# Two units of half products: the second unit's sums of weights made during the first, kept in DRAM, and its additions shared

## The chip, the cores and the metric

One core of one Trainium2 chip runs the whole layer as one program. The metric is the device time of one execution in microseconds (us). Engines are named as in the profile: PE is TensorE (PEld its weight loads), DVE is VectorE, ACT ScalarE, POOL GpSimd, SP SyncE, which here does nothing but issue DMAs ("SPq" is its queue).

## The reference

One layer of a hybrid encoder: D = 1024 channels, T = 1024 + 128 = 1152 tokens. Two branches, an SSD (Mamba-2) branch `y_m` of width 2048 and an attention branch `y_a` of width 1024, are projected to 1024 channels, gated, summed, projected again and normalised:

```python
u = gate_m * jnp.einsum('ble,ed->bld', y_m, w_br_m) + gate_a * jnp.einsum('ble,ed->bld', y_a, w_br_a)
out = jnp.einsum('bld,de->ble', u, w_out)
x_new = layer_norm(DN_ALPHA * x + out, ln_g, ln_b)
```

The change concerns these three lines only, the last 420 us of the kernel. What stands before them (input projection, convolution, scan, attention) is the same in both kernels.

## The kernel before

**Numbers in two halves.** All products are of 32-bit accuracy: each operand is split into a high part `h` (a cast on ACT) and a low part `l` (the difference, on DVE or POOL), and three matmuls (h·h, h·l, l·h) make one product. A matmul is 128 x 128 weights by 384 tokens; the tokens lie in three chunks c0, c1, c2 of 384.

**Order of the last part.** `quarter(A0)`: the first half of `y_a` times its weights. `unit(0)`: rows 4 to 11 of `y_m` (in tiles of 128 rows). `quarter(A1)`: the second half of `y_a`. `unit(1)`: rows 0 to 3 and 12 to 15 of `y_m`. Then the output projection with w_out, chunk by chunk (`out`), with the LayerNorm behind each block.

**A unit** is a product in Strassen's manner. Chunks c0 and c1 and the two halves of the unit's rows make the 2 x 2 blocks; seven products do the work of eight. The blocks of weights for output pair (j1, j2) = (2p, 2p + 1) are B11, B21, B12, B22 and the sums T1, T2, T4, T3; the right sides are A11, A12, A22 and the sums S1 to S4. Chunk c2 is done plainly (D1, D2) with the B pieces. For each p, of which a unit has four (0 to 3 in unit 0; 4 to 7 in unit 1, where the loop variable is again 0 to 3 and the diff says p), that is 11 products of 12 matmuls. So a unit has 528 matmuls. The order of the eight pieces is a table, `ORDERS`, chosen for each p by `PIECES`. The results are added into `acc`, up to four places for one product, on DVE (in unit 0 the first touch of a place is a copy on ACT).

**Weights.** `load_pair` loads the two tiles of 512 KB (B11 and B21; B12 and B22) on SP. `prepare` makes a piece `pc` (1024 wide, high and low half side by side) three pieces ahead of its use: for a T the sum, in place, on DVE (on POOL for the very first p), then the cast on ACT, then the low half on POOL. After T4 and T3 the loads of the next p are issued into the same two raw tiles, so they wait for the POOL subtraction that read them last. `pc` tiles live in the rotating slots `wh` and `wl`, the raw tile B11/B21 in the slot `wr`, which ordinary weights (`fetch`, `split`) use as well.

**What sets the order.** Each engine runs its instructions in the order in which the program lists them, and in the units that is the order of the code (`manual_schedule`). `flow` is a generator ticked every 6 matmuls; its `yield n` waits n ticks. In unit 0 it runs `rows_c01` (loads the second half of `y_a` and splits its chunks c0 and c1 into `ya1hi`, `ya1lo`; `rows_c2` does chunk c2), in quarter 1 `load_sums(1)` (loads unit 1's rows, scales them and makes the sums S), in unit 1 `seconds` (loads the attention product `pa`, its second half and its gate, adds and scales). `final` loads the SSD gate and `finish` multiplies and adds on DVE and POOL; `parts_of_u` splits the merged result into `uhi`, `ulo`; `load_late` and `late` do the same for chunk c2. `load_wo` and `split_wo` load and split the eight rows of w_out; the first two come through `fetch` and `split`. Products of quarter 1 go through a tile `pa` to DRAM (`evac_1`).

Of the kernel before, what the change touches and what calls it, by code (L numbers as in the profile page):

```python
# [19 lines left out]
P = 128  # L20
# [6 lines left out]
CW = 384  # L27
# [122 lines left out]
def trunk_step(ctx: ExitStack, tc: tile.TileContext, I, O):  # L150
# [1194 lines left out]

    def load_sums(v):

# [4 lines left out]
        rb = [None]  # L1352
        pair_ = [send(kts[0], rb, *(() if v else (lazy["f0"], "gs"))), send(kts[1], rb)]
        for i in range(4):
            y0, y1 = pair_
            scaled(kts[2 * i], y0, rb)
            scaled(kts[2 * i + 1], y1, rb)
            if i < 3:
# [24 lines left out]
            if i >= 2:  # L1383
# [4 lines left out]
              ("B11", "B21", "T1", "T2", "B12", "B22", "T4", "T3"))  # L1388
    PIECES = [ORDERS[i] for i in (0, 1, 1, 1, 0, 1, 1, 2)]
    raw = {}  # L1390

    def load_pair(p, which):

        if p % 4 or which >= 2:
            which %= 2
            pool, tag = ((wp, "wr"), (lazy["raw"], "raw"))[which]
            raw[p, which] = t = pool.tile([P, 1024], F32, tag=tag, name=f"wu{p}_{which}", bufs=1)
            sy.dma_start(t[:], I["wbr"][4 + 2 * p + which + 4 * (p // 4)])

    pieces = []  # L1400

    def prepare():

        n = len(pieces)
        if n >= lazy["limit"]:
            return
        p, name = n // 8, PIECES[n // 8][n % 8]
        j1, j2 = raw[p, 0], raw[p, 1]
        b11, b21, b12, b22 = j1[:, 0:512], j1[:, 512:1024], j2[:, 0:512], j2[:, 512:1024]
        out = {"B11": b11, "B21": b21, "B12": b12, "B22": b22, "T1": b11, "T2": b11, "T4": b21, "T3": b12}[name]  # L1410
        if name[0] == "T":
            x, y = {"T1": (b12, b11), "T2": (b22, b11), "T4": (b21, b11), "T3": (b22, b12)}[name]
            (ve if p else po).tensor_tensor(out, x, y, ALU.subtract)  # L1413
        t = wp.tile([P, 1024], F32R, tag=("wh", "wl")[n % 2], name=f"pc{n}")
        ac.copy(t[:, 0:512], out)  # L1415
        po.tensor_tensor(t[:, 512:1024], out, t[:, 0:512].bitcast(F32), ALU.subtract)  # L1416
# [17 lines left out]
    def unit(v, steps):  # L1434

        def to(j, c, d):
            a = acc[:, j, ch(c)]
            if v == 0 and (j, c) not in begun:
                begun.add((j, c))
                ac.copy(a, d)  # L1440
            else:
                ve.tensor_tensor(a, a, d, ALU.add)

        begun = set()
        for p in range(4):
# [11 lines left out]
            for at, piece in enumerate(order):  # L1457
# [51 lines left out]
    lazy["sub"] = po  # L1509
    A1 = [tuple(ap.tile([P, 4, CW], F32R, tag=f"a{x}{c}", name=f"ya1{x}{c}") for x in ("hi", "lo")) for c in range(2)]  # L1510
    ys = []

    def part(i, c):
        h, l = A1[c][0][:, i, :], A1[c][1][:, i, :]
        ac.copy(h, ys[i][:, ch(c)])
        ve.tensor_tensor(l, ys[i][:, ch(c)], h.bitcast(F32), ALU.subtract)

    def rows_c01():

        yield 20  # L1520
        for i in range(4):
            y = mp.tile([P, T], F32, tag="yr", name=f"yr1{i}", bufs=4)
            sy.dma_start(y[:], ya_d[4 + i])
            ys.append(y)
            yield 5
            part(i, 0)
            yield 3
            part(i, 1)
            yield 3

    def rows_c2():

        A1.append(tuple(ap.tile([P, 4, CW], F32R, tag=f"a{x}2", name=f"ya1{x}2") for x in ("hi", "lo")))
        for i in range(4):
            part(i, 2)

    def steps_0(p, piece):

        if p == 3 and piece == "B22":
            flow.after(1, rows_c2)  # L1540

# [77 lines left out]
    def load_wo(*ks):  # L1619

        for k in ks:
            pool, tag = {2: (ap, "ahi1"), 3: (ap, "alo1"), 4: (ap, "ahi0"), 5: (ap, "alo0")}.get(k, (mp, "yr"))
            wraw[k] = pool.tile([P, 1024], F32, tag=tag, name=f"wor{k}", bufs=1 if k < 6 else 4)
            sy.dma_start(wraw[k][:], I["w_out"][k])

    def split_wo(k):

        where = {5: "2", 6: "1", 7: "0"}.get(k)
# [4 lines left out]
        wo.append((hi, lo))  # L1633

    def steps_1(p, piece):

        a, b = 2 * p, 2 * p + 1
        at = PIECES[4 + p].index(piece)
        if p:
            if 1 <= at < 4:  # L1640
                finish(1)
            if at < 4:
                final(((a - 2, 0), (b - 2, 0), (a - 2, 1), (b - 2, 1))[at])
            if at == 4:
                finish(1)
            if at == 6:
                finish(len(pending))
            if at == 7 and p < 3:
                flow.start(seconds(p + 1))
        if p == 2 and at == 0:  # L1650
            load_wo(2, 3)
# [23 lines left out]
    op = ma_stack.enter_context(tc.tile_pool(name="op", bufs=1, reuse_waits="tile"))  # L1675
    last_w = ready.pop(0)
    split()
    wo += [last_w, ready.pop(0)]
    split_wo(2)
    final((6, 1), (7, 1))  # L1680
    gb = xp.tile([P, 2, D], F32, tag="xhi2", name="gb")
    sy.dma_start(gb[:, 0, :], I["ln_g"].to_broadcast([P, D]))
    sy.dma_start(gb[:, 1, :], I["ln_b"].to_broadcast([P, D]))
    for c in range(NCH):
        xr = xp.tile([P, 3, D], F32, tag="xlo2", name=f"xres{c}")
        sy.dma_start(xr[:], I["xt"][3 * c * P:(3 * c + 3) * P].rearrange("(j p) d -> p j d", p=P))
# [7 lines left out]
        def product(j, n, at):  # L1694
# [5 lines left out]
            d = ds[j, n]  # L1700
            (wh, wl), k = wo[at], at
            te.matmul(d[:, :w], uh[:, k, js], wh[:, ns], start=(at == 0), stop=False)
# [3 lines left out]
        if c == 0:  # L1706
            for k in range(8):
                for j, n in blocks:
                    product(j, n, k)
                if k < 5:  # L1710
                    split_wo(k + 3)
                if k == 0:
                    finish(2)
                    load_late(0)
                if k > 1:
                    late(k - 2)
# [116 lines left out]
```

## Time and profile before

| | us |
|---|---|
| median of 3 runs (lowest to highest) | 2038.79 (2038.76 to 2039.94) |
| the profiled execution | 2038.8 |
| its span | 2037.0 |
| quarter 0, 1616.95 to 1666.94 | 49.99 |
| unit 0, to 1758.77 | 91.83 |
| quarter 1, to 1813.80 | 55.03 |
| unit 1, to 1915.66 | 101.86 |
| output c0, c1, c2, to 2029.85 | 41.49, 32.66, 40.04 |
| tail | 7.15 |

The stages are cut where TensorE's matmuls pass from one line of the kernel to the next. In profile lines, `out<-in` are the program's names without their numbers, `x3` is a count, and `[1.18 <-ACT wh L225]` says that the engine had been idle for 1.18 us and what ended that. `L246` is a line of the kernel.

### The profile page before, as it was taken

The numbers are of one execution on the slowest core, as the hardware profiler recorded it, in microseconds if no ns is written. First come the engines' busy times: TensorE is split into PE (matmuls) and PEld (weight loads), VectorE is DVE, ScalarE is ACT, GpSimd is POOL, SyncE is SP. The second block draws the span as 40 slices with busy tenths as digits, with TensorE's granted clock in tenths as the row PEclk, the third lists the DMA queues.
The fourth block names the chain that finished last, engine by engine and source line by source line (L and its number), as shares of the span: only waits on it lengthen the run. The fifth ranks groups of instructions, "written<-read, shape, count | busy, mean of one in ns | idle before, by whom it ended". The sixth has DMA issues, their size and how long they took to land.

```text
span 2037.0 us, 36365 instructions
## 1 busy us (share of the span) xinstructions
PE 2007.6 (99%) x14199; PEld 1858.2 (91%) x14199; DVE 1351.3 (66%) x2233; ACT 949.2 (47%) x2055; POOL 557.8 (27%) x732
## 2 busy tenths in 40 slices
PE   9999999999999999999999999999999999999897
PEld 7899999999999999999888888888988999989786
DVE  4145666666767667643678778777787675577876
ACT  5125455465565555543545554544555453341310
POOL 0012535453545454432010010001001025325610
PEclk9999999999999999999999999999999999999998
DMA  6423242324233332434456665656667662455652
GB/s 221 165 66 97 65 136 79 131 79 128 91 125 91 118 116 82 142 105 164 160 182 214 202 192 192 196 213 198 187 216 207 215 224 100 156 183 196 217 171 93
DMA packets 131691, 311.39 MB, mean 153 GB/s; under 512 B 19528, under 2 KB 78912, under 8 KB 121280
## 3 DMA queue, kind: packets, MB, share of 16 engines
q1 hardware_dynamic: 113936, 217.78, 33.4%
q10 hardware_dynamic: 17584, 91.30, 13.0%
q8 instruction: 111, 1.82, 0.4%
q14 instruction: 60, 0.49, 0.1%
HBM read 243.07 MB, written 65.95 MB: 152 GB/s over the span
## 4 chain that ended last, share of the span: by engine, by line
PE 80%; DVE 9%; DMA 6%; ACT 2%; issue 1%; POOL 1%; SPq 0%; ACTq 0%; DVEq 0%; POOLq 0%
PE d L246 17%; PE d L248 16%; PE d L247 16%; PE s L952 3%; PE o L1027 2%; PE y L737 2%; PE v L336 2%; PE v L335 2%; PE v L334 2%; PE so L1102 1%; PE dS L678 1%; PE y L741 1%; PE ss L1080 1%; PE dq L247 1%; PE dq L246 1%
## 5 line engine op out<-in xcount | busy, mean ns | idle before, releaser
L246 PE MATMUL d<-xh,wh 128*128 128x384 f32 x2112 | 736.2, 349 | 0.0
L248 PE MATMUL d<-xh,wl 128*128 128x384 f32 x2112 | 708.3, 335 | 0.0
L247 PE MATMUL d<-xl,wh 128*128 128x384 f32 x2112 | 707.2, 335 | 0.0
L246 PEld LDWEIGHTS d<-xh,wh 128*128 128x128 f32 x2112 | 396.6, 188 | 19.0 <-issue 7.9
L247 PEld LDWEIGHTS d<-xl,wh 128*128 128x128 f32 x2112 | 397.2, 188 | 0.8
L248 PEld LDWEIGHTS d<-xh,wl 128*128 128x128 f32 x2112 | 396.4, 188 | 0.0
L226 POOL TENSOR_TENSOR wl<-wr,wh 128x1024 fp32r<-128x1024 f32 x37 | 89.0, 2404 | 189.1 <-ACT wh L225 189.1
L1416 POOL TENSOR_TENSOR pc<-wu,pc 128x512 fp32r<-128x512 f32 x64 | 87.9, 1381 | 172.8 <-ACT pc L1415 172.8
L957 ACT ACTIVATE st<-s,ckt 128x256 f32<-128x256 f32 (+1 forms) x320 | 115.1, 467 | 19.6 <-PE s L952 17.3
L1017 ACT ACTIVATE st<-st 128x1024 f32<-128x1024 f32 x80 | 83.1, 1062 | 41.6 <-DVE st L1012 38.4
L961 POOL TENSOR_TENSOR st<-st,mask_bf 128x256 f32<-128x256 f32 x64 | 48.8, 783 | 194.4 <-ACT st L957 194.3
L706 ACT ACTIVATE m<-ce,nacum 128x128 f32<-128x128 f32 x288 | 96.8, 391 | 5.7 <-PE y L737 5.7
L1415 ACT CAST pc<-wu 128x512 fp32r<-128x512 f32 x64 | 38.5, 622 | 116.8 <-DVE wu L1413 88.9
L229 DVE SCALAR_TENSOR_TENSOR wl<-wr,wh 128x1024 fp32r<-128x1024 f32 x50 | 62.1, 1242 | 32.5 <-ACT wh L228 32.4
L633 POOL TENSOR_TENSOR wx<-xdt,wdt 128x256 f32<-128x256 f32 x72 | 54.0, 751 | 84.9 <-DVE xdt L631 84.9
L225 ACT CAST wh<-wr 128x1024 fp32r<-128x1024 f32 x48 | 50.3, 1049 | 53.7 <-PE d L247 43.9
L1027 PE MATMUL o<-st,vt 128*64 128x256 f32 (+1 forms) x640 | 68.9, 362 | 0.9 <-ACT st L1017 0.4
L1027 PEld LDWEIGHTS o<-st,vt 128*64 128x64 f32 x640 | 43.4, 137 | 26.7 <-ACT st L1017 4.0
L852 ACT ACTIVATE gate<-d,bcol 128x384 f32<-128x384 f32 x48 | 27.7, 578 | 71.9 <-PE d L248 46.7
L686 POOL TENSOR_TENSOR S<-S,ea 128x256 f32<-128x256 f32 x56 | 37.8, 674 | 75.9 <-DVE S L687 64.6
L1038 DVE TENSOR_TENSOR st<-st 128x1024 f32<-128x1024 f32 (+1 forms) x40 | 57.4, 1436 | 0.8
L228 ACT ACTIVATE wh<-wr 128x1024 fp32r<-128x1024 f32 x50 | 52.7, 1054 | 10.7 <-PE d L247 10.7
(906 smaller groups left out, 4324.8 us busy)
## 6 DMA issues: line engine op xcount, KB each, us to landing
wr<-in_wt SPq DMA_DIRECT2D x88, 512.0 KB
kc<-in_cache_k ACTq DMA_DIRECT2D x32, 1024.0 KB
vc<-in_cache_v ACTq DMA_DIRECT2D x32, 1024.0 KB
ce<-ac_d SPq DMA_DIRECT2D x96, 192.0 KB
sb<-cs_d ACTq DMA_DIRECT2D x16, 576.0 KB
yr<-ym_d SPq DMA_DIRECT2D x16, 576.0 KB
gate_d<-gate SPq DMA_DIRECT2D x45, 192.0 KB
s<-in_state_ssm SPq DMA_DIRECT2D x8, 1024.0 KB
```

Of the source, the lines that this page charges most:

```text
L226: lazy.get("sub", po).tensor_tensor(lo[:, :cols], raw[:, :cols], hi[:, :cols].bitcast(F32), ALU.subtract)
L229: ve.scalar_tensor_tensor(lo[:, :cols], raw[:, :cols], scale, hi[:, :cols].bitcast(F32), ALU.mult, ALU.subtract)
L246: te.matmul(out, wh, xh, start=(k == 0), stop=False)
L247: te.matmul(out, wh, xl, start=False, stop=False)
L248: te.matmul(out, wl, xh, start=False, stop=(k == n - 1))
L706: ac.activation(m[:, j, :], ce[:, j * P:(j + 1) * P], AF.Abs, bias=nacum[:, b, h:h + 1])
L952: te.matmul(ps2[:, e, 256 * x + q0:256 * x + 256], kk[hr, ks], qq[hr, qs], start=(at == 0), stop=(at == 2))
L957: ac.activation(S[j][:, e, kb, q0:], ps2[:, e, 256 * x + q0:256 * x + 256], AF.Identity, bias=ckt[:, kb, 2 * hp + e:2 * hp + e + 1])
L1017: ac.activation(w, w, AF.Exp, scale=-1.0)
L1027: te.matmul(o[64 * e:64 * e + 64, 256 * at + q0:256 * at + 256], vt[:, kb, 64 * e:64 * e + 64], S[j][:, e, kb, q0:256], start=(kb == 0), s ...
L1038: ve.tensor_tensor(s[:, :, 0:h, :], s[:, :, 0:h, :], s[:, :, 2 * n - h:2 * n, :], ALU.add)
L1416: po.tensor_tensor(t[:, 512:1024], out, t[:, 0:512].bitcast(F32), ALU.subtract)
```

## The change

- `sums_of_weights`, the first thing that `rows_c01` now does, runs during unit 0. For p = 4 to 7 it loads both tiles of weights again (`we`, into slots `yr`), makes the four sums on DVE, casts on ACT into tiles `te`, makes the low halves on DVE, and stores each sum (512 KB) to the new DRAM tile `t_d`. In unit 1 `prepare` loads the T pieces from `t_d` straight into `pc`; B pieces are made as before.
- The raw tiles' second half (B12, B22) is now two tiles of 512 columns, `wv`, loaded by two DMAs. In unit 1 the loads of the next p are issued after B21 and B22 instead of T4 and T3.
- In unit 1 A11's product is added to one place, and copied on ACT to `shared`; T2's and T3's products are added to `shared`, and `shared` to the places. That makes 13 additions on DVE instead of 16 for each p. PIECES has order 1 instead of order 0 for p = 4.
- `rows_c2` is called directly after B22 of the last p of unit 0, ahead of `split()`; before, it came one tick into T3. Right after it come the first two loads and scalings of unit 1's rows (`first_rows(1)`), formerly in quarter 1.
- `evac_1` takes turns among four buffers instead of two.
- In unit 1 and the output the loads and splits of w_out, `final`, `finish`, `late` and `parts_of_u` are placed anew; rows of w_out are used in the order 0, 2, 1, 3 to 7; `parts_of_u` of c1 and c2 come in c0 and c1.

```diff
+    t_d = dr.tile([16, P, 1024], F32, name="t_d")
...
+    def sums_of_weights():
+        early = {}
+        for p in range(4, 8):
+            for j, names in enumerate((("B11", "B21"), ("B12", "B22"))):
+                t = mp.tile([P, 1024], F32, tag="yr", name=f"we{p}_{j}", bufs=4)
+                sy.dma_start(t[:], weights_of(p, j))
+                early[p, names[0]], early[p, names[1]] = t[:, 0:512], t[:, 512:1024]
+            if p == 4:
+                yield 4
+            for i, n in enumerate(SUMS):
+                x = sum_of(early, p, n, ve)
+                o = ap.tile([P, 1024], F32R, tag=("ahi0", "alo0", "ahi1", "alo1")[i], name=f"te{p}_{i}")
+                ac.copy(o[:, 0:512], x)
+                ve.tensor_tensor(o[:, 512:1024], x, o[:, 0:512].bitcast(F32), ALU.subtract)
+                sy.dma_start(t_d[4 * (p - 4) + i], o[:].bitcast(F32))
+                yield 3
...
     def prepare():
...
-        ac.copy(t[:, 0:512], out)
-        po.tensor_tensor(t[:, 512:1024], out, t[:, 0:512].bitcast(F32), ALU.subtract)
+        if p >= 4 and name in SUMS:
+            sy.dma_start(t[:].bitcast(F32), t_d[4 * (p - 4) + SUMS.index(name)])
+        else:
+            out = sum_of(raw, p, name, ve if p else po) if name in SUMS else raw[p, name]
+            ac.copy(t[:, 0:512], out)
+            po.tensor_tensor(t[:, 512:1024], out, t[:, 0:512].bitcast(F32), ALU.subtract)
...
                 elif piece == "T2":
-                    step(piece, "S2", "m6", True, True, (j2, 0), (j1, 1), (j2, 1))
+                        step(piece, "S2", "m6", True, True)
+                        ve.tensor_tensor(shared, shared, A["m6"], ALU.add)
+                        put_on(shared, (j2, 0))
...
         if p == 3 and piece == "B22":
-            flow.after(1, rows_c2)
+            flow.drain()
+            rows_c2()
+            lazy["rows"] = first_rows(1)
...
     def evac_1(j, c, d):
-        t = mp.tile([P, CW], F32, tag="gt", name=f"pa{j}_{c}", bufs=2)
+        n = 3 * j + c
+        if n % 2:
+            t = mp.tile([P, CW], F32, tag="gt", name=f"pa{j}_{c}", bufs=2)[:]
+        else:
+            t = lazy["raw"].tile([P, 512], F32, tag=f"raw{n // 2 % 2}", name=f"pa{j}_{c}", bufs=1)[:, 0:CW]
...
             if at == 3:
                 parts_of_u(0, (2, 3))
+                final((a, 0), (b, 0))
             if at == 4:
-                parts_of_u(0, (4,))
+                parts_of_u(0, (4, 5))
             if at == 5:
-                parts_of_u(0, (5,))
                 flow.drain()
-                final((a, 0), (b, 0))
-            if at == 6:
-                load_wo(4, 5, 6, 7)
-                parts_of_u(0, (6, 7))
+                finish(2)
+                load_wo(4, 5)
+                final((a, 1), (b, 1))
```

How this moves instructions is seen on three queues. In the rows below a piece is numbered through (`pc8` is B11 of p1, `pc9` B21, `pc10` T1, `pc11` T2, `pc12` T4, `pc13` B12), and `te5_0` is T1 of p = 5. First ACT in unit 0, around p1, before:

```order
L1415 CAST pc8_18414<-wu1_0_18364 128x512 [waits DMAHW7_49,PE_49,Activation_49]
L1415 CAST pc9_18433<-wu1_0_18364 128x512 [waits PE_49,Activation_49]
L1415 CAST pc10_18451<-wu1_0_18364 128x512 [waits DVE_49,PE_49]
L1415 CAST pc11_18472<-wu1_0_18364 128x512 [waits DVE_49,PE_49]
L1515 CAST ya1hi0_18260<-yr10_18461 128x384 [waits DMAHW1_49]
L1440 COPY acc_17604<-u01m1_18488 128x384 [waits PE_49]
L1440 COPY acc_17604<-u01m1_18488 128x384 x3
L1415 CAST pc12_18508<-wu1_0_18364 128x512 [waits DVE_49,Pool_49]
```

and now:

```order
L1457 CAST pc8_18439<-wu1_18377 128x512 [waits DMAHW3_49,PE_49,Activation_49]
L1439 CAST te5_0_18454<-we5_0_18449 128x512 [waits DMAHW0_49,DMAHW1_49,DVE_49,Activation_49]
L1457 CAST pc9_18467<-wu1_18377 128x512 [waits PE_49,Activation_49]
L1439 CAST te5_1_18484<-we5_0_18449 128x512 [waits DMAHW2_49,DVE_49]
L1457 CAST pc10_18489<-wu1_18377 128x512 [waits DVE_49,PE_49,Activation_49]
L1457 CAST pc11_18508<-wu1_18377 128x512 [waits DVE_49,PE_49]
L1439 CAST te5_2_18520<-we5_0_18449 128x512 [waits DMAHW4_49,DVE_49]
L1439 CAST te5_3_18544<-we5_1_18451 128x512 [waits DMAHW5_49,DMAHW1_49,DVE_49]
L1483 COPY acc_17605<-u01m1_18530 128x384 [waits PE_49]
L1483 COPY acc_17605<-u01m1_18530 128x384 x3
L1457 CAST pc12_18552<-wu1_18377 128x512 [waits DVE_49,Pool_49]
```

The four `te5` casts stand among p1's own; further down `te6_0` stands ahead of `pc13` in the same way. The second queue is SP at the same place. Before, it held only loads of `wu` and `yr` there; now:

```order
L1411 DMA wu1_18377<-in_wbr 128x1024 [waits DMAHW3_49,Pool_49]
L1441 DMA t_d_80<-te4_2_18386 128x1024 [waits DMAHW4_49,DVE_49]
L1441 DMA t_d_80<-te4_3_18411 128x1024 [waits DMAHW5_49,DVE_49]
L1416 DMA wv1_0_18420<-in_wbr 128x512 [waits DMAHW6_49,Pool_49]
L1416 DMA wv1_1_18422<-in_wbr 128x512 [waits DMAHW7_49]
L1432 DMA we5_0_18449<-in_wbr 128x1024 [waits DMAHW0_49]
L1432 DMA we5_1_18451<-in_wbr 128x1024 [waits DMAHW1_49]
L1441 DMA t_d_80<-te5_0_18454 128x1024 [waits DMAHW2_49,DVE_49]
L1441 DMA t_d_80<-te5_1_18484 128x1024 [waits DMAHW3_49,DVE_49]
L1441 DMA t_d_80<-te5_2_18520 128x1024 [waits DMAHW4_49,DVE_49]
L1441 DMA t_d_80<-te5_3_18544 128x1024 [waits DMAHW5_49,DVE_49]
L1411 DMA wu2_18556<-in_wbr 128x1024 [waits DMAHW6_49,Pool_49]
```

The `we5` loads stand behind the `wv1` loads; `we6` follows `wu2` in the next rows. The third is ACT at the end of unit 0, before:

```order
L1415 CAST pc31_18974<-wu3_1_18786 128x512 [waits DVE_49,PE_49]
L1440 COPY acc_17604<-u03d2_18993 128x384 [waits PE_49]
L225 CAST wh92_19033<-wr92_18991 128x1024 [waits DMAHW1_49,Pool_49]
L1515 CAST ya1hi2_19046<-yr10_18461 128x384 [waits PE_49]
L1515 CAST ya1hi2_19046<-yr11_18558 128x384
L1515 CAST ya1hi2_19046<-yr12_18662 128x384
L1515 CAST ya1hi2_19046<-yr13_18759 128x384
```

and now:

```order
L1457 CAST pc31_19086<-wv3_0_18877 128x512 [waits DVE_49,PE_49]
L1483 COPY acc_17605<-u03d2_19106 128x384 [waits PE_49]
L1596 CAST ya1hi2_19146<-yc10_18839 128x384 [waits DMAHW7_49,PE_49]
L1596 CAST ya1hi2_19146<-yc11_18906 128x384 [waits DMAHW3_49]
L1596 CAST ya1hi2_19146<-yc12_18961 128x384 [waits DMAHW5_49]
L1596 CAST ya1hi2_19146<-yc13_19021 128x384 [waits DMAHW7_49]
L226 CAST wh92_19164<-wr92_19104 128x1024 [waits DMAHW0_49,Pool_49]
```

`wh92` is the high half of quarter 1's first weights; it has passed behind the four `ya1hi2` casts.

More of the change, by code (lines that the diff above doesn't have):

```diff
@@ L1388, in trunk_step, with weights_of, sum_of @@
               ("B11", "B21", "T1", "T2", "B12", "B22", "T4", "T3"))
-    PIECES = [ORDERS[i] for i in (0, 1, 1, 1, 0, 1, 1, 2)]
+    PIECES = [ORDERS[i] for i in (0, 1, 1, 1, 1, 1, 1, 2)]
+    SUMS = ("T1", "T2", "T4", "T3")
     raw = {}
+    def weights_of(p, which):
+        return I["wbr"][4 + 2 * p + which + 4 * (p // 4)]
     def load_pair(p, which):
[L1394 to L1398, printed above, removed]
+        if which == 0:
+            t = wp.tile([P, 1024], F32, tag="wr", name=f"wu{p}", bufs=1)
+            sy.dma_start(t[:], weights_of(p, 0))
+            raw[p, "B11"], raw[p, "B21"] = t[:, 0:512], t[:, 512:1024]
+        else:
+            for i, n in enumerate(("B12", "B22")):
+                t = lazy["raw"].tile([P, 512], F32, tag=f"raw{i}", name=f"wv{p}_{i}", bufs=1)
+                sy.dma_start(t[:], weights_of(p, 1)[:, 512 * i:512 * i + 512])
+                raw[p, n] = t[:]
+    def sum_of(r, p, name, eng):
+        out, x, y = {"T1": ("B11", "B12", "B11"), "T2": ("B11", "B22", "B11"), "T4": ("B21", "B21", "B11"),
+                     "T3": ("B12", "B22", "B12")}[name]
+        eng.tensor_tensor(r[p, out], r[p, x], r[p, y], ALU.subtract)
+        return r[p, out]
+    def sums_of_weights():
[14 more added lines that the diff above has]
+                yield 3
     pieces = []
@@ L1442, in to, with put_on @@
                 ve.tensor_tensor(a, a, d, ALU.add)
+        def put_on(src, *jcs):
+            for j, c in jcs:
+                a = acc[:, j, ch(c)]
+                ve.tensor_tensor(a, a, src, ALU.add)
         begun = set()
@@ L1494, in sums_last @@
     def sums_last(v):
+        if v:
+            load_pair(4, 1)
         prepare()
@@ L1638, in steps_1 @@
         at = PIECES[4 + p].index(piece)
[L1639 to L1645, printed above, removed]
-            if at == 6:
[L1647 to L1651, printed above, removed]
+        if at >= 6 and p < 3:
+            final((a, at - 6))
+        if p and at < 4:
+            if at < 2:
+                final((b - 2, at))
+            finish(1)
+        if at == 5 and 0 < p < 3:
+            flow.start(seconds(p + 1))
+        if p == 0 and at == 4:
+            load_wo(2)
+        if p == 1 and at == 4:
+            split_wo(2)
+            load_wo(3)
         if p == 3:
@@ L1675, in trunk_step @@
     op = ma_stack.enter_context(tc.tile_pool(name="op", bufs=1, reuse_waits="tile"))
-    last_w = ready.pop(0)
+    wo[0] = ready.pop(0)
+    finish(2)
     split()
-    wo += [last_w, ready.pop(0)]
-    split_wo(2)
-    final((6, 1), (7, 1))
+    wo[1] = ready.pop(0)
+    split_wo(3)
+    load_wo(6)
+    parts_of_u(0, (6, 7))
+    load_late(0)
+    rows_of_wo = (0, 2, 1, 3, 4, 5, 6, 7)
     gb = xp.tile([P, 2, D], F32, tag="xhi2", name="gb")
@@ L1709, in trunk_step @@
                     product(j, n, k)
[L1710 to L1716, printed above, removed]
+                if k < 4:
+                    split_wo(k + 4)
+                if k == 2:
+                    load_wo(7)
+                if k % 2:
+                    late(k // 2)
+            parts_of_u(1, range(8))
         for j in range(3):
             if c == 1 and j < 2:
-                late(6 + j)
+                late(4 + 2 * j)
+                late(5 + 2 * j)
+            if c == 1 and j == 2:
+                parts_of_u(2, range(8))
             b, w = 3 * c + j, width[j]
```

116 lines of the change are left out of this document (66 added, 50 removed).

## The prediction

> **What bounds the kernel now.** I read the head of the page first: TensorE is busy for nearly the whole span, so a gain or a loss can only come from time in which it waits or runs at a reduced clock.
>
> ```profile
> span 2037.0 us, 36365 instructions
> PE 2007.6 (99%) x14199; PEld 1858.2 (91%) x14199; DVE 1351.3 (66%) x2233; ACT 949.2 (47%) x2055; POOL 557.8 (27%) x732
> ```
>
> The view of waits gives TensorE's waits by line; all but a fraction lie after 1758 us. The stage windows (the columns are time, busy us of each engine with its instructions, granted clock, DMA share and GB/s) show what surrounds them. In order: first quarter, first unit, second quarter, second unit, then the output projection's chunks c0, c1, c2.
>
> ```profile
> PE out L1702 <- ACT wh L228: 6.5, 1, 6.5
> PE out L1704 <- DVE ulo L1617: 3.5, 2, 2.9
> PE u11d L1430 <- POOL pc L1416: 3.0, 3, 1.4
> PE dq L248 <- POOL wl L226: 1.8, 1, 1.8
> PE dq L246 <- ACT wh L225: 1.2, 1, 1.2
> PE u13m L1430 <- POOL pc L1416: 1.1, 1, 1.1
> ```
>
> ```profile
> 1616.95:1666.94 49.99, 49.99 (x291) 49.99 (x290) 40.40 (x63) 28.83 (x62) 2.55 (x2) 1.00 0.79 270
> 1666.94:1758.77 91.83, 91.83 (x529) 91.83 (x529) 39.86 (x66) 36.86 (x75) 47.49 (x35) 1.00 0.25 85
> 1758.77:1813.80 55.03, 52.04 (x289) 51.40 (x289) 44.66 (x62) 26.93 (x56) 10.44 (x5) 0.97 0.73 239
> 1813.80:1915.66 101.86, 95.03 (x529) 91.13 (x528) 77.04 (x113) 26.40 (x50) 57.21 (x43) 1.00 0.52 177
> 1915.66:1957.15 41.49, 34.98 (x145) 28.69 (x145) 26.75 (x41) 10.07 (x13) 13.33 (x8) 0.92 0.61 202
> 1957.15:1989.81 32.66, 32.66 (x146) 27.04 (x144) 29.69 (x56) 5.66 (x12) 4.25 (x4) 1.00 0.60 196
> 1989.81:2029.85 40.04, 36.52 (x193) 31.24 (x191) 26.35 (x51) 1.70 (x5) 0.25 (x1) 0.91 0.25 92
> ```
>
> Equal work stands in pairs here. The quarters differ by 55.03 − 49.99 = 5.0 us, the units by 101.86 − 91.83 = 10.0, c0 and c1 by 41.49 − 32.66 = 8.8. In c2 the wait is 3.5 and the reduced clock takes 0.09 × 36.5 = 3.3, together 6.8. So at most 30.6 us can be won after unit 0, and nothing in it: unit 0 has no waits at all, and can only lose. DVE has 52 us free in unit 0 and 25 in unit 1; the change moves work from the second to the first.
>
> **A wait costs more than itself.** In quarter 1:
>
> ```profile
> 1797.56 0.44 PE L246 MATMUL dq<-ya1hi,wh 128*128 128x384 f32 x1 [1.18 <-ACT wh L225]
> 1799.99 0.44 PE L248 MATMUL dq<-ya1hi,wl 128*128 128x384 f32 x1 [1.81 <-POOL wl L226]
> 1800.00:1804.00 4.00, 4.00 (x14) 4.00 (x15) 3.97 (x6) 2.21 (x5) 0.00 (x0) 0.57 0.54 182
> ```
>
> After 3.0 us of waiting the granted clock is 0.57 over the next 4 us, which loses 0.43 × 4 = 1.7 us; the quarter's excess of 5.0 leaves 2.0 beside the 3.0. I take 1.9. The Trainium skill (TensorE: Matmul & The Clock Gate, section "Why this matters for your kernels") asks for no idle gap over about 3 us; here two gaps of 1.18 and 1.81 us were enough. By that rule the short wait at quarter 1's start, below, would have no slow tail, and the sum would be 1.9 us lower; the trace speaks for the tail.
>
> **Part 1, unit 0: sums for unit 1 beside its own.** Added for each p of 4 to 7: two loads of 512 KB, four sums and four low halves on DVE, four casts on ACT, four stores of 512 KB on SP. It is the order that I doubt. Times u below count from the unit's start, 1666.94. One product of 12 matmuls takes 91.83 / 44 = 2.087, so piece p1 begins at u 22.9, B21(p1) at 27.1, T4(p1) at 35.5, B12(p1) at 37.6.
>
> ```profile
> 1683.24 3.60 SPq L1398 DMA_DIRECT2D wu<-in_wbr  x2
> 1685.19 1.29 POOL L1416 TENSOR_TENSOR pc<-wu,pc 128x512 fp32r<-128x512 f32 x1 [0.73 <-ACT pc L1415]
> 1686.99 1.14 ACT L1415 CAST pc<-wu 128x512 fp32r<-128x512 f32 x2 [1.88 <-DMA wu<-in_wbr]
> 1685.89 1.48 DVE L1442 TENSOR_TENSOR acc<-acc,u00m 128x384 f32<-128x384 f32 x3 [1.03 <-PE u00m L1430]
> 1690.01 0.78 DVE L1413 TENSOR_TENSOR wu<-wu,wu 128x512 f32<-128x512 f32 x1 [1.49 <-DMA wu<-in_wbr]
> 1696.00 0.68 DVE L1413 TENSOR_TENSOR wu<-wu 128x512 f32<-128x512 f32 x1
> 1696.77 0.62 ACT L1415 CAST pc<-wu 128x512 fp32r<-128x512 f32 x1 [0.55 <-DVE wu L1413]
> 1697.47 1.29 POOL L1416 TENSOR_TENSOR pc<-wu,pc 128x512 fp32r<-128x512 f32 x1 [1.80 <-ACT pc L1415]
> ```
>
> With the sums' 0.7 and the cast's 0.62 of these rows the added work is 32 × 0.7 = 22 us of DVE (52 free) and 16 × 0.62 = 10 of ACT (55 free); the DMA share of 0.25 has room too. By volume all of it hides.
>
> The first load was issued at 1683.24 and used at 1686.99: 3.75 us. The second went out when POOL finished T3(p0) at 1686.48 (u 19.5) and was used at 1690.01: 3.5. T4(p1) was summed at u 29.1 and its POOL part ended at u 31.8.
>
> Now the loads `we` of p=5 stand in SP's queue behind the two `wv` loads, which wait for that POOL end. With the added ACT cast ahead of T3's I put it at u 20.6, four issues later `we` goes out at about 21.7, and with the `wv` loads, its twin and two stores beside it, 2.5 MB in all, I let it take 4.5 and land at L = 26.2 (at best 19.5 + 0.3 + 3.5 = 23.3). ACT runs in order, and `te5_0` stands ahead of B21(p1)'s cast: sum 0.7, cast 0.62 and B21's cast 0.62 end at 28.1; its POOL part at 29.5; needed at 27.1 and 27.5. Loss about 2.
>
> DVE then has, before T4(p1)'s sum: four sums and four low halves (0.7 each), the four casts that stand between them on ACT (0.75 with handing over), six additions to `acc` (0.5), three sums (0.7 with T4's), and about 1.2 of waiting for POOL before T1 overwrites B11. That is 5.6 + 3.0 + 3.0 + 2.1 + 1.2 = 14.9, of which I let 1.0 overlap: T4(p1) is summed at L + 13.9 = 40.1 instead of 29.1, and POOL is done with it 0.1 + 0.62 + 0.08 + 1.29 + about 0.3 later, at 42.5. TensorE wanted it at 35.5. Worse, that POOL end releases SP's load `wu2`, behind which the `we` loads of p=6 stand; issued at 43.4, used at 47.3; and ACT has `te6_0` ahead of B12(p1)'s cast. Cast at 49.2, POOL part at 50.6, wanted at 37.9 (u 37.6 and the first two matmuls' 0.35). So TensorE has lost 12.7 by then, plus one slow tail of 1.9, and by the same chain another 1 or so at T4(p2). By p3 nothing more stands in the way. Term: **+15**. The bounds: with L = 23.3, T4's POOL part at 39.6 and `te6_0` in front, B12's POOL part comes at 47.7, which is 10 + 1.9. If T4 kept its old end at 31.8, `we6` would go out at 32.7, and B12 be ready at 39.9, for a loss of 2 plus 2 at B21, about 5 with the tail. At the top, each of p5, p6 and p7 could lose 6 to 8: 22. I take 15, since the issue and the in-order wait both follow from rows.
>
> **Part 2, quarter 1's start.** Before, `wh` was cast ahead of the four `ya1hi` casts; now it stands behind them, as `rows_c2` comes right after B22.
>
> ```profile
> 1755.15 1.05 ACT L225 CAST wh<-wr 128x1024 fp32r<-128x1024 f32 x1
> 1756.33 2.42 POOL L226 TENSOR_TENSOR wl<-wr,wh 128x1024 fp32r<-128x1024 f32 x1 [3.65 <-ACT wh L225]
> 1756.85 1.76 ACT L1515 CAST ya1hi<-yr 128x384 fp32r<-128x384 f32 x4 [0.65 <-PE u03m L1430]
> 1758.77 0.34 PE L246 MATMUL dq<-ya1hi,wh 128*128 128x384 f32 x1
> ```
>
> The four casts start when TensorE is through with `u03m`, as before at 1756.85, and end at 1758.61, so `wh` comes at 1759.7 and `wl` at 1759.7 + 2.42 = 1762.1. Wanted at 1758.77 and 0.35 later: TensorE idles 0.9 and, after two matmuls, 2.1. With the tail **+5.0** (3.0 without it; 5.5 if ACT also gets there late). Later in the quarter the 1.18 + 1.81 and their tail go, since `wh` no longer stands behind copies `pa` that wait for their stores: now four buffers instead of two, and the first rows are loaded in unit 0. **−5.1** (0 if the yr loads are the limit).
>
> **Part 3, unit 1.** Per p, T1 to T4 lose 4 sums (DVE 0.75), 4 casts (ACT) and 4 POOL halves, and DVE makes 13 additions of 0.54 instead of 16, ACT one copy more. DVE falls by 4 × (4 × 0.75 + 3 × 0.54) = 18.5 of 77, POOL by 16 × 1.34 = 21 of 57. In their place come 16 loads of 512 KB, 8.4 MB on top of 18.
>
> ```profile
> L1442 DVE TENSOR_TENSOR acc<-acc,u11m 128x384 f32<-128x384 f32 x14 | 7.1, 545 | 1.4 <-PE u11m L1430 1.4
> L1416 POOL TENSOR_TENSOR pc<-wu,pc 128x512 fp32r<-128x512 f32 x64 | 87.9, 1381 | 172.8 <-ACT pc L1415 172.8
> L1590 POOL TENSOR_TENSOR acc<-acc,pa 128x384 f32<-128x384 f32 x16 | 24.4, 1531 | 19.7 <-DVE acc L1589 19.7
> 1863.65 3.41 DMA wu<-in_wbr
> DMA packets 7716, 18.05 MB, mean 177 GB/s; under 512 B 859, under 2 KB 3719, under 8 KB 7710
> GB/s 199 265 147 84 0 31 182 95 32 212 382 358 69 170 198 35 336 66 6 13 316 345 418 66 35 403 373 95 0 145 387 385 65 58 224 182 0 66 361 279
> ```
>
> The last three are a load of 512 KB in the chain, 3.41 us, and the traffic of unit 1, whole and in 40 slices. (18.05 + 8.4) MB in 92 us is 287 GB/s, and single slices reached 418, so the loads fit in the mean. Their issue waits for a piece slot, two pieces or at least 4.2 us ahead of use, against 3.41 to 3.75: 0.4 us of slack at the tightest. B pieces still go through POOL, behind `finish` additions of 1.5 each that wait on DVE. I leave 2 of the 10.0: **−8** (−10 if all goes, +4 if six of the sixteen loads come 2.3 late each).
>
> **Part 4, output.** The 6.5 us wait of the first matmuls for `wh`, the first half of w_out, came since its load stood behind the last T sums; T2 and T4 of p7 now need no `wr` slot, and the load is issued after B21(p7). It is there some 5 us early. **−8.8** (−5 if the second half, 1.3 us early by my count, becomes late). In c2, `ulo` is now made in c1, ahead of the LayerNorm of the last block of c1: **−6** of 6.8 (0 if the c1 additions hold DVE so long).
>
> **Sum.** 2038.8 (span 2037.0 and 1.8 around it; the median of the runs is 2038.79) + 15 + 5.0 − 5.1 − 8 − 8.8 − 6 = 2030.9. Forecast 2031, its own range 2023 to 2038.
>
> **Rivals.** A, unit 0 hides all. ACT reaches `te` only when its data are there; for it speaks the DMA share of 0.25 and DVE's 52 free us, against it the order of SP and ACT. Then 2038.8 − 22.9 (the others) = 2016. Chance 0.19.
> B, slower: unit 0 loses more than the rest wins. The chain at T4(p1) and B12(p1) comes again at p2 and p3, since each `we` load waits behind a `wu` load that POOL releases late. From a loss of 27 (22.9 + 4.1) it is slower; 12.7 + 1.9 and two of 7 make 28.6, so 2038.8 − 22.9 + 28.6 = 2044.5. For it: the order repeats with `te7`; against it: after p1 SP has its `wv` loads ahead of `we7`, and TensorE itself is late, so that the data catch up. Chance 0.18.
> C, about no change: unit 0 loses 15 to 18, and of the gains only quarter 1 and c0 come whole, unit 1 wins 3 and c2 nothing, as the 16 loads come late: 2038.8 + 16 + 5 − 5.1 − 3 − 8.8 = 2043, or 2037 with c2's 6. Taken at 2039. Chance 0.15.
> The forecast has the remaining 0.48.
>
> The measurement tells 0.2% (4.1 us) from no change: same is 2034.7 to 2042.9. Of the forecast's 0.48 I put 0.42 below it and 0.06 in it; with A faster is 0.61, with C same is 0.21, B is 0.18. The range from 2015 to 2043 takes in A and C and the bounds of part 1, and leaves out B and little more.
>
> **What the profile after would show.** Right: unit 0 at about 107 us with waits of TensorE on ACT and POOL `pc` at B21, T4 and B12 of p1; quarter 1 at 55 with a wait on `wh` at its very start and none at its fourth weights; unit 1 near 94; no wait of `out` on `wh`; c2 near 34. Unit 0 under 95 means that A holds; waits in unit 1 on `pc` from the DMA of `t_d` mean C; waits in p2 and p3 of unit 0 mean B. I would be wrong most easily in L and in what DVE does between it and T4(p1).

## The result, and the profile after

The changed kernel takes 2061.56 us (median of 4 runs, 2058.32 to 2066.38) against 2039.37 before (4 runs, 2038.76 to 2040.88). The ratio is 1.011, with an interval of 1.0087 to 1.0132: slower by 22 us, where 2031 had been forecast. The profiled execution took 2066.38 us, so its stages lose some 5 us more than the median does. The head of its page, then TensorE's waits (us in total, times, longest):

```profile
span 2064.6 us, 36468 instructions
PE 2021.1 (98%) x14199; PEld 1867.5 (90%) x14199; DVE 1355.0 (66%) x2237; ACT 951.5 (46%) x2059; POOL 541.5 (26%) x716
```

```profile
PE u01d L1471 <- ACT pc L1457: 8.8, 2, 6.1
PE u02m L1471 <- ACT pc L1457: 6.1, 2, 3.1
PE u12m L1471 <- DMA pc<-t_d: 3.8, 2, 3.2
PE dq L249 <- POOL wl L227: 2.0, 1, 2.0
PE out L1777 <- ACT uhi L1689: 1.7, 1, 1.7
```

Unit 0 (`u0..`), which had no wait, now has the largest ones, all on pieces `pc`. The stage windows, cut as before (quarter 0, unit 0, quarter 1, unit 1, c0, c1, c2):

```profile
1617.13:1667.05 49.92, 49.92 (x290) 49.92 (x289) 40.97 (x62) 28.93 (x62) 2.55 (x2) 1.00 0.78 270
1667.05:1795.69 128.64, 107.33 (x529) 101.41 (x528) 66.60 (x101) 45.06 (x91) 46.38 (x34) 0.88 0.48 173
1795.69:1849.63 53.94, 51.92 (x289) 51.60 (x290) 41.17 (x58) 29.27 (x60) 13.49 (x6) 0.97 0.64 210
1849.63:1950.29 100.66, 94.61 (x529) 93.15 (x529) 60.95 (x90) 18.03 (x33) 37.01 (x28) 0.98 0.78 271
1950.29:1985.18 34.89, 33.27 (x145) 26.90 (x145) 21.19 (x35) 9.56 (x15) 11.74 (x5) 1.00 0.63 204
1985.18:2017.82 32.64, 32.64 (x145) 27.04 (x144) 29.48 (x57) 5.14 (x11) 3.58 (x4) 1.00 0.57 191
2017.82:2057.29 39.47, 36.70 (x193) 31.27 (x191) 27.44 (x51) 2.21 (x6) 1.98 (x2) 0.91 0.31 109
```

Against before: unit 0 +36.8, quarter 1 −1.1, unit 1 −1.2, c0 with the wait ahead of it −6.6, c2 −0.6, the tail (7.3 us) +0.2. That is +27.5 of the span's +27.6; the loss lies in unit 0. Its 36.8 us are 20.6 of waits on pieces, 107.33 − 91.83 = 15.5 of matmuls that ran slowly, and 0.7 of waiting for quarter 1's first `wh`, which falls ahead of the cut. Unit 0 repeats well: four later kernels with the same early sums took 126.6 to 129.6 us there. Rows picked from the timeline around the two largest waits show where they come from (SPq is the issue of a DMA; SP and the engines at the place, then TensorE):

```profile
1690.39 0.82 SPq L1416 DMA_DIRECT2D wv<-in_wbr  x2
1691.27 0.90 SPq L1432 DMA_DIRECT2D we<-in_wbr  x2
1698.94 0.69 DVE L1423 TENSOR_TENSOR we<-we,we 128x512 f32<-128x512 f32 x1 [8.33 <-DMA we<-in_wbr]
1699.70 0.62 ACT L1439 CAST te<-we 128x512 fp32r<-128x512 f32 x1 [9.20 <-DVE we L1423]
1700.23 0.61 ACT L1457 CAST pc<-wu 128x512 fp32r<-128x512 f32 x1
...
1700.89 0.69 PE L1471 MATMUL u01d<-ym0h,pc 128*128 128x384 f32 x1 [2.74 <-ACT pc L1457]
...
1714.29 1.27 POOL L1458 TENSOR_TENSOR pc<-wu,pc 128x512 fp32r<-128x512 f32 x1 [3.92 <-ACT pc L1457]
1715.59 0.33 SPq L1411 DMA_DIRECT2D wu<-in_wbr  x1
1715.97 0.90 SPq L1432 DMA_DIRECT2D we<-in_wbr  x2
1721.80 0.69 DVE L1423 TENSOR_TENSOR we<-we,we 128x512 f32<-128x512 f32 x1 [8.29 <-DMA we<-in_wbr]
1722.57 0.62 ACT L1439 CAST te<-we 128x512 fp32r<-128x512 f32 x1 [7.97 <-DVE we L1423]
1723.09 0.61 ACT L1457 CAST pc<-wv 128x512 fp32r<-128x512 f32 x1
...
1723.76 0.69 PE L1471 MATMUL u01d<-ym0h,pc 128*128 128x384 f32 x1 [6.11 <-ACT pc L1457]
```

Read it from the bottom of each group: TensorE waits for a cast `pc` (B21, then B12 of p1), whose own data had long been there; ACT stands at the cast `te` listed ahead of it; that waits for DVE's early sum, and DVE for a load that went out 7.7 and 5.8 us before. DVE's waits for these loads over unit 0 stand in one row, three waits for p = 5, 6 and 7:

```profile
DVE we L1423 <- DMA we<-in_wbr: 23.0, 3, 8.3
```

So the theory, called Q in the expectations: the early sums have engine time enough, and lose it to queues that run in order behind late loads. Its rival V: the engines and the DMA have too much to do side by side, wherever the loads stand.

### The profile page after: what moved, and what is told of

It reads as the page before. It is cut to its first block, busy times and chain, and to the rows that moved or that the text cites. A ratio compares the mean times of both kernels' runs of the same rounds, so it can differ in the third digit from the quotient of the medians.

```text
span 2064.6 us, 36468 instructions
## 1 busy us (share of the span) xinstructions
PE 2021.1 (98%) x14199; PEld 1867.5 (90%) x14199; DVE 1355.0 (66%) x2237; ACT 951.5 (46%) x2059; POOL 541.5 (26%) x716
## 4 chain that ended last, share of the span: by engine, by line
PE 76%; DVE 9%; DMA 6%; issue 3%; POOL 3%; ACT 2%; SPq 0%; ACTq 0%; DVEq 0%; POOLq 0%
PE d L247 17%; PE d L249 16%; PE d L248 16%; PE s L953 3%; PE o L1028 2%; PE y L738 2%; PE v L337 2%; PE v L336 2%; PE v L335 2%; PE so L1103 1%; PE dS L679 1%; POOL pc L1458 1%; PE y L742 1%; PE ss L1081 1%; PE dq L249 1%
## 5 line engine op out<-in xcount | busy, mean ns | idle before, releaser
L1458 POOL TENSOR_TENSOR pc<-wu,pc 128x512 fp32r<-128x512 f32 x28 | 37.5, 1348 | 140.2 <-ACT pc L1457 140.2
L336 PE MATMUL v<-vl,xh 128*128 128x512 f32 x144 | 56.4, 391 | 0.4 <-DVE vl L329 0.4
```

Source lines behind the costliest of these rows:

```text
L336: te.matmul(d, xh, wl, start=False, stop=False)
```

## Experiments in unit 0: order or volume

Each ratio below is to the kernel before in the same round of runs, whose median lay between 2038.4 and 2040.3 us. Each stage time is from one profiled execution.

**Without the early sums.** Unit 1 makes its T pieces itself again; the loads of the next p come after T4 and T3 again.

```diff
-        yield from sums_of_weights()
+        yield 20
...
-        if p >= 4 and name in SUMS:
-            sy.dma_start(t[:].bitcast(F32), t_d[4 * (p - 4) + SUMS.index(name)])
```

> The sums for unit 1 are not made in unit 0 any more: unit 1 makes its T pieces itself, as before the change. All the rest of the change stays (shared additions, quarter 1's start, the order of the output). Theory Q (the loss comes from queues that run in order behind late loads of weights for the early sums): unit 0 returns to 92 us, unit 1 stays near 100, so 2061.5 - 33 = 2028, between 2023 and 2035. Rival R (another part of the change, the rows loaded early for quarter 1 and unit 1, delays unit 0): unit 0 stays above 105 and the time above 2045.

Measured: 2034.81 us (10 runs), ratio 0.9975 (0.9965 to 0.9986). Its unit 0 and unit 1:

```profile
1664.50:1757.65 93.15, 92.30 (x530) 91.66 (x529) 38.49 (x67) 35.60 (x73) 44.39 (x34) 1.00 0.30 108
1811.57:1918.08 106.51, 98.40 (x530) 96.05 (x529) 78.25 (x104) 25.97 (x47) 59.02 (x42) 0.95 0.52 178
```

Unit 0 is back, R has fallen. The time is at the upper end of what was expected, since unit 1 takes 106.5 us, not 100. DVE is busy there for 78.3 us, as before the change (77.0) and not as in the changed kernel (61.0): it is the sums in DRAM that relieve it. The additions themselves took less there (26.6 us instead of 30.0 before the change), but the multiplications of `finish` took 1.12 us each instead of 0.81, and one split of w_out (1.5) has come; what the shared additions are worth by themselves isn't shown.

**The loads one p ahead.** The same loads, sums and stores, with the two loads for p + 1 ahead of the sums of p:

```diff
+        load_early(4)
+        yield 4
         for p in range(4, 8):
-            for j, names in enumerate((("B11", "B21"), ("B12", "B22"))):
-                ...
-            if p == 4:
-                yield 4
+            if p < 7:
+                load_early(p + 1)
```

> The early sums stay, but the two tiles of weights for the next p are loaded before the sums of this p, one p (12 ticks, 12.5 us) ahead of use; as many loads, sums and stores as in the changed kernel. Theory Q: the waits of 8.3, 8.3 and 6.4 us of DVE for these loads go, and with them ACT's, so unit 0 takes 95 to 108 us instead of 128.6, and the whole 2030 to 2045. Rival V (unit 0 is slow by volume: DVE and POOL disturb each other and the DMA engines are full): unit 0 stays above 118 and the time above 2052.

Measured: 2038.47 us (10 runs), ratio 1.000 (0.999 to 1.001); unit 0:

```profile
1666.51:1772.00 105.49, 96.49 (x529) 92.65 (x529) 67.16 (x99) 44.61 (x90) 47.46 (x34) 0.98 0.60 211
```

DVE, ACT and POOL do the same work as in the changed kernel (67.16, 44.61 and 47.46 us against 66.60, 45.06 and 46.38), and more is moved in each us; unit 0 is 23 us shorter. V has fallen for these 23 of 36.8. Some 12 us over the 93.2 without early sums remained. Their largest wait was 2.85 us for T3 of p2, whose sum stands on DVE behind a `ya1lo` split that waits for ACT, which waits for the first row of y_a.

**Two more edits of order.** The rows of y_a are loaded one ahead, and the low half of a sum comes one tick after its cast:

```diff
                 ac.copy(o[:, 0:512], x)
+                yield 1
                 ve.tensor_tensor(o[:, 512:1024], x, o[:, 0:512].bitcast(F32), ALU.subtract)
                 sy.dma_start(t_d[4 * (p - 4) + i], o[:].bitcast(F32))
-                yield 3
+                yield 2
...
+        load_row(0)
+        yield 6
         for i in range(4):
+            if i < 3:
+                load_row(i + 1)
...
```

> The kernel with the loads one p ahead, and two more edits of order in unit 0, with the same work: DVE makes the low half of an early sum one tick after ACT's cast instead of directly behind it (DVE stood 0.7 us for each of 16 casts), and the rows of the second half of y_a are loaded one row ahead (ACT stood 6.2 us for the first). Theory Q (order of queues): unit 0 falls from 105.5 to 94 to 99 us, the whole to 2026 to 2033. Rival V (the rest, some 12 us over the 93.2 without the early sums, is what their volume on DVE, ACT, POOL and DMA costs): unit 0 stays at 103 or above, and the whole within 2 us of 2038.5.

Measured: 2030.16 us (4 runs), ratio 0.9962 (0.9947 to 0.9977).

```profile
1666.92:1763.71 96.79, 93.36 (x529) 91.44 (x528) 67.51 (x101) 44.96 (x91) 47.88 (x34) 1.00 0.65 230
```

With the volume untouched, 31.8 of the 36.8 us are gone. That order, not volume, made unit 0 slow is shown for these; 3.6 us over the 93.2 without early sums remain, and this run doesn't say what they are.

## Experiments behind unit 0

**Quarter 1's start.**

```diff
             flow.drain()
-            rows_c2()
+            flow.after(1, rows_c2)
             lazy["rows"] = first_rows(1)
```

> The changed kernel with one edit: the splits of chunk c2 (rows_c2) come one tick into T3 again, behind the split of quarter 1's first weights. The step of the prediction: quarter 1 loses its two waits of 0.7 and 2.0 us and the slow clock behind them, 53.9 becomes about 49.5 to 50.5, and the whole falls by 4, to 2057 or 2058. Rival: the wait goes to the ya1hi splits, which are now the late ones, and quarter 1 stays at 53 or above. The runs of the changed kernel spread over 8 us, so the stage tells this, not the whole.

Measured: 2061.00 us (4 runs; the spread hides the 4 us); quarter 1 is undisturbed, with no wait left:

```profile
1795.97:1845.89 49.92, 49.92 (x290) 49.92 (x289) 41.36 (x62) 28.67 (x60) 13.23 (x5) 1.00 0.63 211
```

So the wait of 2.0 us and the slow clock cost 53.94 − 49.92 = 4.0, and with the wait of 0.7, which lies ahead of the cut, the start cost 4.7, as the step had it (5.0).

**Unit 1's loads from DRAM by ACT's queue.**

```diff
-            sy.dma_start(t[:].bitcast(F32), t_d[4 * (p - 4) + SUMS.index(name)])
+            ac.dma_start(t[:].bitcast(F32), t_d[4 * (p - 4) + SUMS.index(name)])
```

> The changed kernel with one edit: the T pieces of unit 1 are loaded by ACT's queue instead of SP's, where they stand behind loads that wait for DVE. Theory Q, for unit 1: the waits of 3.25, 1.57 and 0.50 us on these loads go, unit 1 falls from 100.7 to 93 to 96, and the whole by 5 to 7, to about 2055. Rival V: the loads are late since the DMA engines are full (some slices of unit 1 moved over 400 GB/s), so the waits stay, and unit 1 stays at 99 or above.

Measured: 2063.99 us (4 runs), unit 1 102.1 us. The expectation of Q was missed: the waits on `t_d` stayed and the longest became 5.4 us. ACT stands in order as well: the load of that piece went out at 1906.66, right behind ACT's copy to `shared`, which had waited 17.8 us for DVE's addition. So only the queue that waits was exchanged. The Trainium skill (DMA: Bandwidth & Descriptors, section "Issuing engines are not separate DMA queues") has it that another issuing engine saves issue time alone, since all use the same DMA engines. This run gained nothing either, but by ACT's own wait, so it isn't a test of that rule. The chain in unit 1 of the changed kernel shows for what DVE waits (start, us, what; pieces under 0.4 us are left out, and one issue):

```profile
1897.68 5.99 DMA pb<-pa_d
...
1903.80 0.96 DVE pa L1644
1904.76 0.47 DVE sh L1545
...
1905.26 1.03 DVE acc L1491 x2
1906.28 0.88 DVE pa L1646
...
1907.54 0.43 SPq L1642
...
1908.54 4.87 DMA pc<-t_d
```

DVE waits for the attention half's load (`pa_d`), SP for DVE, and T4's load goes out only then; TensorE wanted it at 1911 and got it at 1914.5.

**Half of each T piece.** Unit 1 loads the high halves only and multiplies them twice; the low halves of the T pieces are left out of the result.

> The changed kernel, but unit 1 loads only the high half of each T piece (256 KB instead of 512, 4.2 MB less in unit 1) and multiplies it twice, so the number of matmuls stays and the low half of the T pieces is left out of the result. The order of all queues stays. Theory V for unit 1 (the loads come late since the DMA engines are full at the start of each p): the waits on pc from t_d fall from 5.3 us to under 2, and unit 1 from 100.7 to 96 or less. Rival Q (they are issued late, behind loads that wait for DVE): the waits fall by no more than the 1.3 us that 256 KB less take at 400 GB/s for each late load, and unit 1 stays at 98 to 101. The whole, between 2054 and 2062, spreads too much to tell it; the stage does.

Measured: 2055.59 us (4 runs), ratio 1.0089 (1.0069 to 1.0110), which overlaps that of the changed kernel. The waits on `t_d` fell from 5.3 to 2.2 us (1.57 to 0.97, 3.25 to 0.91, 0.50 to none, and two new ones of 0.2).

```profile
1849.88:1947.39 97.51, 94.17 (x530) 91.47 (x529) 59.89 (x90) 17.95 (x33) 37.69 (x28) 1.00 0.70 239
```

97.5 falls within neither V's 96 or less nor Q's 98 to 101. (256 KB at 400 GB/s are 0.66 us, not the 1.3 of the expectation.) One profile can't tell it: unit 1 with the full loads and the same code took 97.2 to 105.6 us in the six profiles that have it, with 2.6 to 9.4 us of waits on `t_d`. What the bytes cost in unit 1 stays open.

**The late additions at their old rate** (`late` from k = 2 on in c0, one with each of two blocks of c1):

```diff
-                if k % 2:
-                    late(k // 2)
+                if k > 1:
+                    late(k - 2)
```

> The changed kernel with one edit: the additions of chunk c2 (late) have their old rate again, six in c0 and one with each of two blocks of c1, instead of four in c0 and two with each; the splits of c2 stay at the last block of c1. Theory: c2's waits on uhi and ulo (1.7 and 1.1 us and the slow clock behind) stem from the last late additions, which come 2 to 4 us after the LayerNorm of c1's blocks on DVE; then c2 falls from 39.5 to about 35. Rival: DVE is held by the LayerNorm anyway, and c2 stays above 38.

Measured: 2058.03 us (4 runs); c2 34.6 us as expected, the wait on `uhi` gone and 0.85 left on `ulo`. The output from c0 to c2, 107.0 us in the changed kernel's profile:

```profile
1947.96:2049.96 102.00, 99.34 (x481) 83.25 (x480) 77.13 (x141) 17.19 (x32) 17.26 (x10) 1.00 0.52 174
```

The profiles of the other runs weaken this in size. With the output's code unchanged, c2 took 37.0 to 39.5 us with both waits in five profiles, the changed kernel's among them, but 33.7 and 33.4 with neither in the two with ACT's queue and with half pieces. With this edit it took 34.3 to 36.0 in four, never with a wait on `uhi`. So the edit takes away a wait that comes in most executions, not in all.

**All edits, and then the attention halves.** The three edits in unit 0 with the two just shown:

> The kernel with the three edits of order in unit 0 (2030.2 us), with the splits of c2 behind those of quarter 1's first weights, and with the late additions at their old rate. Theory Q: each of the two edits gives here what it gave alone, 4.0 in quarter 1 (53.9 to 49.9) and 4 to 5 in the output (106.7 to 102.0), so 2021 to 2023. Rival: quarter 1 and the output have other limits once unit 0 no longer holds them, and the whole stays above 2026.

Measured: 2025.59 us (4 runs), ratio 0.9922 (0.9907 to 0.9937). That lies between the two expectations, nearer to the rival's. Quarter 1 took 49.9 us and the output 103.2, about as expected; the profile shows what is missing in unit 1, which took 105.6 us, with 9.4 us of waits on `t_d`. Unit 1's code is the same here as in the changed kernel; its five other profiles had 97.2 to 102.8 us.

The next edit is in unit 1:

```diff
             sy.dma_start(t, gate_d[8 + j][:, 0:2 * CW])
-            yield 5
+            yield 7
```

> The same, and in unit 1 the additions of the attention halves come 7 ticks behind their loads instead of 5. Theory: DVE waits up to 6.8 us for these loads, and SP, which waits for DVE before the next of them, holds the loads of the T pieces behind; with the data there when DVE comes, unit 1 falls from 99 to 94 to 96 and the whole to 3 or 4 under the kernel with 5 ticks. Rival V (the DMA engines are full at the start of each p, whatever waits for what): unit 1 stays within 1.5 us.

Measured: 2020.24 us (4 runs), ratio 0.990 (0.9885 to 0.9915). DVE's waits for the attention halves in unit 1, with 5 ticks:

```profile
DVE pa L1658 <- DMA pb<-pa_d: 29.3, 7, 8.1
```

and with 7, followed by its unit 0 and unit 1:

```profile
DVE pa L1658 <- DMA pb<-pa_d: 11.6, 5, 5.2
```

```profile
1666.05:1761.34 95.29, 93.23 (x529) 91.63 (x529) 65.85 (x96) 44.80 (x90) 49.96 (x35) 1.00 0.67 234
...
1811.27:1906.95 95.68, 92.82 (x529) 91.65 (x529) 59.41 (x89) 17.86 (x33) 35.96 (x28) 1.00 0.82 292
```

DVE waits 18 us less, and unit 1 is 10 us shorter than with 5 ticks in that pair, moving 292 GB/s against 266. The pair overstates it, since the profile with 5 ticks is of the longest of its four executions; the medians differ by 5.4 us. Still, 95.7 and the 93.7 of the next run, which has 7 ticks as well, lie below all six profiles with 5 (97.2 to 105.6). So in unit 1 too the place of a wait counts, with the same bytes; `t_d` waits of 2.9 us are left, and how many of them are V's isn't shown.

**A later start of the early sums,** the same, with 7 ticks, and `yield 8` for the first `yield 4` (the expectation says 5 ticks, but the kernel that ran has 7):

> As the kernel with 5 ticks, and the first early sum comes 8 ticks after unit 0's start instead of 4. In p0 POOL makes its own sums, and a DVE sum beside it took 1.4 to 1.8 us instead of 0.7, and POOL's 1.7 instead of 1.3. Theory: the later start moves some of these apart, the waits of 0.9 and 0.7 us for T3 of p0 shrink, unit 0 falls by 1 to 3 us from 96.8. Rival: the last sums and the rows of y_a then crowd at the unit's end, and unit 0 is 97 to 100.

Measured: 2022.04 us (4 runs), not to be told from 2020.24; unit 0 97.9 us against 95.3. The waits of p0 went, but waits of 0.5 to 0.8 us on POOL halves grew in p1 and came in p2 and p3: unit 0 is where the rival had it.

The version with 7 ticks has the lowest median of all: 1.0% below the kernel before, some 2% below the changed one.

## Why the prediction was wrong

What happened is its rival B, which had 0.18, and the place was the one named: the `we` loads behind `wv` and `wu` on SP, `te5_0` ahead of B21 and `te6_0` ahead of B12 on ACT. B's own sum did not come: it gave 2044.5, 17 us under the 2061.56, and had the chain of T4 and B12 come again at p2 and p3, where p2 lost at T1 and T3 and p3 nothing. The sign named for C, waits in unit 1 on `t_d`, came too (5.3 us). Term by term:

- **Unit 0, +15 forecast, +36.8 measured.** The waits of p1 came near: 2.74 + 0.35 at B21, 1.21 + 0.72 at T4, 6.11 + 0.34 at B12, 11.5 together against 12.7. Three sub-steps failed. First and largest, "one slow tail of 1.9": slow matmuls took 15.5. Five separate stalls had a tail each. The windows behind them, with granted clock 0.50 to 0.68, lose busy time times what the clock lacks of 1, about 10 of the 15.5 us; most of the rest lies right behind these windows. The stall at T4(p1), 1.21 and 0.72, had none: its matmuls ran at 1.00 until the next wait (the third row):

```profile
1689.06:1693.60 4.54, 3.79 (x12) 3.47 (x13) 1.54 (x4) 0.62 (x1) 2.56 (x2) 0.68 0.92 318
...
1700.89:1705.60 4.71, 4.36 (x12) 3.85 (x13) 4.03 (x9) 0.63 (x2) 1.28 (x1) 0.50 0.37 147
...
1712.70:1717.30 4.60, 2.67 (x14) 2.01 (x13) 0.81 (x2) 1.90 (x5) 1.27 (x1) 1.00 0.41 165
...
1723.76:1728.50 4.74, 4.39 (x13) 3.89 (x14) 3.91 (x7) 1.14 (x2) 2.56 (x2) 0.53 0.40 165
...
1746.11:1750.80 4.69, 4.35 (x12) 3.84 (x13) 3.45 (x5) 1.72 (x4) 1.80 (x2) 0.50 0.33 136
...
1766.22:1771.00 4.78, 4.43 (x13) 3.93 (x14) 0.00 (x0) 0.99 (x2) 3.74 (x3) 0.50 0.46 128
```

- Second, "another 1 or so at T4(p2)": T4(p2) lost 0.6, but p2 as a whole 7.4 us of waits. `te7_0` stood ahead of T1's sum and cast, and its load took 6.0 us from issue (2.98 + 0.34); T3's sum and cast stood behind a split of y_a that waited for its row (3.12 + 0.34). The second is an in-order wait of the same kind that the working never priced:

```profile
1742.22 0.69 DVE L1423 TENSOR_TENSOR we<-we,we 128x512 f32<-128x512 f32 x1 [6.36 <-DMA we<-in_wbr]
...
1746.11 0.69 PE L1471 MATMUL u02m<-ym0h,pc 128*128 128x384 f32 x1 [2.98 <-ACT pc L1457]
...
1761.89 0.93 ACT L1596 CAST ya1hi<-yr 128x384 fp32r<-128x384 f32 x2 [6.47 <-DMA yr<-ya_d]
...
1766.22 0.69 PE L1471 MATMUL u02m<-S3h,pc 128*128 128x384 f32 x1 [3.12 <-ACT pc L1457]
```

- Third, p0 lost 1.75, put at nothing: T3's cast stood on ACT behind that of an early sum, which DVE made in 1.77 us beside POOL instead of 0.7.
- The load time L, the value said to be the weakest, was off: sums at u 31.9, not L = 26.2 (u from this profile's start of unit 0, 1667.05). The load went out at u 24.2 instead of 21.7 and took 7.7 us instead of 4.5. So T4's POOL half was done at u 48.5 instead of 42.5 and B12's at 58.0 instead of 50.6. That p1's waits came out so near all the same is luck: TensorE, held by its waits and its slow clock, came to both pieces later as well.
- **Quarter 1's start, +5.0**: 4.7, by the run that undoes it, 0.7 of it counted in unit 0. **Its fourth weights, −5.1**: right, no wait is left there; 53.94 − 49.92 is the start alone.
- **Unit 1, −8 forecast, −1.2 measured** (−4.6 to +3.8 in five other profiles of the same code). "The loads fit in the mean" was right and beside the point: a T piece's load took 4.9 us behind a full start of p, not 3.4 to 3.75, and its issue stood behind a wait of SP for DVE. The bound of +4 for late loads covers this.
- **Output.** Of the −8.8 at c0, 6.6 came: the wait for `wh` is gone, and one of 1.4 for `wl` has come. Of −6 in c2 only 0.6 came in this profile; the others with this output had −1.9 to −6.6. I priced the splits' new place and not the additions' new rate, though the changes to the kernel have both.

So the mechanism was right and the chain was followed too short. Of what unit 0's waits and slow matmuls lost beyond the working's 12.7 + 1.9 + 1, 13.6 us are the slow clock, counted once, 6.4 the waits of p2 and 1.75 those of p0; p1 came 1.2 below. The working stopped at the chain's second link, though the order that it had read repeats with `te7`. Of the Trainium skill's rule (TensorE: Matmul & The Clock Gate, section "Why this matters for your kernels": no idle gaps over about 3 us), the runs show both sides: 1.00 and 0.75 us, one after the other, brought a clock of 0.50 between 1691 and 1693 in one profile, and 0.94 and 0.74 at the same place brought none in the run with the three edits (clock 1.00 in its unit 0). What decides between the two isn't shown.

## What to carry to other kernels

Free engine time says that work can be added, not that it can be added in that place: look at what stands directly behind each added instruction on its engine, and at the load that it waits for, and give that load a full buffer's lead. Moving the loads ahead turned a loss of 22 us into none, and five further moves of order into a gain of 20, with the same work. Reckon with a slow clock for every stall of the matmul engine that is separate from the last, not once for a chain; here five of the six stalls over 1 us in unit 0 had one, of about 2 to 3 us each.

## What the hardware showed beside that

- **A load's time under traffic.** Two loads of 512 KB issued at 1691.27 were in use at 1698.94, and two at 1715.97 at 1721.80; in the kernel before, such a load took 3.4 to 3.75 us.
- **DVE and POOL beside each other.** In p0 of unit 0 both engines make sums, and both are slower while they overlap; without POOL beside it the same DVE instruction takes 0.68:

```profile
1685.55 1.74 POOL L1423 TENSOR_TENSOR wv<-wv,wv 128x512 f32<-128x512 f32 x1
1686.06 1.77 DVE L1423 TENSOR_TENSOR we<-we 128x512 f32<-128x512 f32 x1
...
1710.85 0.68 DVE L1423 TENSOR_TENSOR we<-we 128x512 f32<-128x512 f32 x1
```

The Trainium skill (SBUF — State Buffer, section "Terms") has it that the two engines take turns at a port pair under a lock, and that the loser waits for the whole instruction. These rows agree: 1.77 is 0.68 and 1.09 of waiting, less than one POOL instruction of 1.3. It isn't so for every pair of instructions: three additions to `acc`, which add a product of TensorE, took 1.48 us from 1689.13 beside a POOL subtraction of 1.29 from 1689.08, neither longer than by itself.
